# Adaptive-modulation weights laid out by output feature: a VectorE multiply-and-sum per 128 features instead of a VectorE multiply-add per input block with a TensorE column sum

## The chip, the core and the metric

The kernel runs on one core of one Trainium2 chip. The metric is the device time of one execution in microseconds (us). PE is TensorE, DVE is VectorE, ACT is ScalarE, POOL is GpSimd, and SP is the engine whose queue issues nearly all DMAs.

## What is computed

Two layers of a decoder trunk on 256 tokens of width 1024. Each layer takes six vectors of 1024 values from a conditioning vector `c`, and uses them as shift, scale and gate of its two sub-layers:

```
mod = silu(c) @ ada_w[l] + ada_b[l]        # ada_w[l]: 1024 x 6144, float32
h = RMSNorm(x) * (1 + scale_m) + shift_m
... mixer: one projection h @ w_in[l], three branches (RWKV-7, SSD, FoX), merged @ w_out[l]
x = x + gate_m * merged
h = RMSNorm(x) * (1 + scale_f) + shift_f
x = x + gate_f * FFN(h)                    # layer 0 dense SwiGLU, layer 1 top-2-of-8 experts
```

Only the first line is computed in another way after the change. Everything is float32. A product that needs full precision is made of three matmuls on a high and a low part.

## The kernel before

**The big products.** All weights stream from HBM through a ring of three 1 MB tiles `raw` (`raw_piece`, `load_raw`). Each piece of `raw` is split by ACT into `hi` (L156) and by DVE into `lo = raw - hi` (L157, `split_part`), and PE multiplies both with the split activations (`mm3`). So each projection needs DVE before PE, and a ring slot is free for the next DMA once DVE has read it. A mixer layer runs projections, recurrent scan and attention interleaved by the table `ORDER`; then follow `project_out`, and the dense FFN (layer 0) or the experts (layer 1). The scan of `rwkv_half` begins with 32x32 transposes on DVE (L654). What stands before them on DVE is needed first.

**The modulation.** 48 parts of 128 features a layer, 6 vectors of 8. The weights come as the reference has them, input feature by row. The first two vectors of layer 0 (scale and shift of the mixer) are needed before anything else: `first_load` brings them in eight DMAs of 1 MB, and `first_half` multiplies them on PE with `silc` (silu of `c`, one column per 128 inputs) in groups, brings the result to SBUF with ACT, and sums over partitions with four matmuls against `ones` of one column each; `mod_put` adds the bias. The other 20 halves (512 features each) are spread over the program by `mod_next`, which the steps `mo` and `md` of `ORDER` call, and `ffn` after each of its steps: `mod_load` issues the DMAs (tile `araw`, two buffers; for `md` eight tiles of the ring `u` at once), `mod_add`/`mod_sum` makes eight DVE operations of 128x512 on one accumulator, the first a TENSOR_SCALAR (L223), then seven SCALAR_TENSOR_TENSOR (L225), and `mod_finish` sums the accumulator over partitions on PE by four one-column matmuls against `ones` and adds the bias. Six of the halves lie in layer 0's mixer, nine in the FFN, five in layer 1's mixer. The accumulators of the mixer layers are tiles of the ring `u` (15 buffers), which the scan and the attention use too.

**What sets the order.** The code is traced in program order; then a scheduler chooses the order on each engine, within the dependencies and the buffers that are free. Each engine and SP's queue then run strictly in that order.

Of the kernel before, what the change touches and what calls it, by code (L numbers as in the profile page):

```python
# [63 lines left out]
def trunk(  # L64
    ctx: ExitStack, tc: tile.TileContext,
    x, cols, heads, dtw, ada_w, w_in, lora_up, lora_g, rw_v_down, rw_v_up, proj_rw, proj_ssd, proj_fox, w_out,
# [117 lines left out]
    silc = const("silc", [P, KD])  # L184
    cth = const("cth", [P, KD])
    act.activation(cth, pcol[:, 0:KD], AF.Tanh, scale=0.5)
    dve.scalar_tensor_tensor(cth, cth, 1.0, pcol[:, 0:KD], op0=ALU.add, op1=ALU.mult)
    dve.tensor_scalar_mul(silc, cth, 0.5)
# [4 lines left out]
    def mod_put(l, part, half, ps):  # L193
        o = part * 8 + half * 4
        return dve.tensor_tensor(mods[l][part][:, half * 4:half * 4 + 4], ps, adab[l][:, o:o + 4], op=ALU.add)

    mod_raw, mod_late, norm_end = [], [], []

    def mod_load(sc, deep):

        l, part, half = mod_queue.pop(0)
        c0 = part * D + half * 512
        raws = []
        for k0 in range(0, KD, 1 if deep else 2):
            if deep:
                raw = sc("u", [P, 1, 512], bufs=NUNIT)
            else:
                raw = sc("araw", [P, 2, 512], bufs=2)
            with tc.issue_after(loads[2].ins):
                nc.sync.dma_start(raw, rows(ada_w[l], k0 * P, raw.shape[1] * P, c0, 512))  # L210
            raws += [raw[:, i, :] for i in range(raw.shape[1])]
        mod_raw.append((raws, (l, part, half)))

    def mod_add(sc, raws, key):

        with tc.issue_after(norm_end[-1].ins):
            mod_sum(sc, raws, key)

    def mod_sum(sc, raws, key):
        for kt, raw in enumerate(raws):  # L220
            if kt == 0:
                acc = sc("u", [P, 512], bufs=NUNIT) if sc is mx else sc("macc", [P, 512], bufs=3)
                dve.tensor_scalar_mul(acc, raw, silc[:, kt:kt + 1])  # L223
            else:
# [14 lines left out]
    FIRST = [(p, h) for p in (1, 0) for h in range(2)]  # L239
    araws, last_raw = [], []  # L240

    def first_load(n):
        p, h = FIRST[n // 2]
        raw = raw_piece(4, 512) if n < 3 or n == 7 else mx("b8", [P, 4, 512], bufs=NB8)
        last_raw.append(nc.sync.dma_start(raw, rows(ada_w[0], (n % 2) * 512, 512, p * D + h * 512, 512)))
        araws.append(raw)

    def first_half(n):
        ps = sbank()
        for kg in range(2):  # L250
            for q in range(4):
                mm(ps[32 * q:32 * q + 32, :], silc[:, 4 * kg + q:4 * kg + q + 1].broadcast_to([P, 32]), araws[2 * n + kg][:, q, :], kg == 0, kg == 1)
        acc = mx("u", [P, 512], bufs=NUNIT)
        act.activation(acc, ps, AF.Copy, scale=1.0 / 32)
        ps = dbank()
        for j in range(4):
            mm(ps[:, j:j + 1], acc[:, j * P:(j + 1) * P], ones[:, 0:1])
        return mod_put(0, *FIRST[n], ps[:, 0:4])

# [22 lines left out]
    def load_lora(l):  # L282
        up = keep("up", [P, 2, RW])
        nc.sync.dma_start(up, lora_up[l].rearrange("p (a w) -> p a w", a=2))
        gu1 = keep("gu1", [32, RW])
        nc.sync.dma_start(gu1, lora_g[l])
        return up[:, 0, :], up[:, 1, :], gu1

    mod_queue = [(l, p, h) for l, parts in ((0, (2, 4, 3, 5)), (1, (1, 0, 2, 4, 3, 5))) for p in parts for h in range(2)]

    def mod_next(sc, left, deep=False):
        if len(mod_late) > 1:
            mod_finish(mbank if sc is mx else sbank)
        if deep and mod_raw:
            mod_add(sc, *mod_raw.pop(0))
        if len(mod_queue) > left:
            mod_load(sc, deep)
        if not deep and mod_raw:
            mod_add(sc, *mod_raw.pop(0))

    def mod_flush(sc):
        while mod_raw:
            mod_add(sc, *mod_raw.pop(0))
        while mod_late:
            mod_finish(mbank if sc is mx else sbank)
# [153 lines left out]
    def rwkv(mx, l, prm, lora):  # L459
        pp, pph, omu, c2 = prm["pp"], prm["pph"], prm["omu"], prm["c2"]  # L460
        wa = mx("wa", [P, T], bufs=1 + (l > 0))
        gl = mx("gl", [P, 2, T], bufs=1 + (l > 0))
# [548 lines left out]
    def ffn(ff, w_gu, w_down, gf):  # L1011
# [30 lines left out]
        for s in range(steps):  # L1042
# [4 lines left out]
            if s == 8:  # L1047
                mod_flush(ff)
# [449 lines left out]
```

## Time and profile before

| | |
|---|---|
| three runs | 2223.58, 2232.92, 2234.73 us (median 2232.92) |
| profiled execution | 2224.52 us, its span 2222.8 us |
| busy PE / DVE / ACT / POOL | 95% / 81% / 62% / 7% of the span |
| DMA | 546.68 MB, 246 GB/s mean |
| stages in the span | start to 35, layer 0 mixer to 500, FFN to 700, layer 1 mixer to 1175, experts to the end |

A busy share is an average over stages with different limits. What matters for an edit is which engine another waits for in the stage where the edit falls, so the stages are read one by one. An engine works through its queue in order: an instruction that stands in front of another delays it even where nobody needs the first one yet.

### The profile page before, as it was taken

The numbers are of one execution on the slowest core, as the hardware profiler recorded it, in microseconds if no ns is written. First come the engines' busy times: TensorE is split into PE (matmuls) and PEld (weight loads), VectorE is DVE, ScalarE is ACT, GpSimd is POOL, SyncE is SP. The second block draws the span as 40 slices with busy tenths as digits, with TensorE's granted clock in tenths as the row PEclk, the third lists the DMA queues.
The fourth block names the chain that finished last, engine by engine and source line by source line (L and its number), as shares of the span: only waits on it lengthen the run. The fifth ranks groups of instructions, "written<-read, shape, count | busy, mean of one in ns | idle before, by whom it ended". The sixth has DMA issues, their size and how long they took to land.

```text
span 2222.8 us, 35724 instructions
## 1 busy us (share of the span) xinstructions
PE 2115.0 (95%) x13489; PEld 1811.2 (81%) x13489; DVE 1798.8 (81%) x2822; ACT 1386.1 (62%) x2204; POOL 152.1 (7%) x180
## 2 busy tenths in 40 slices
PE   7899899999998889989998999999999999999998
PEld 4777789998997877868998788888888887888776
DVE  4977776777776797756768999999999989999887
ACT  3454455555454545434555877878878777878775
POOL 2211200000000031211002000000000000000000
PEclk9999999999999998988998999999999999999999
DMA  8423254667884533414556999999999999999994
GB/s 304 128 83 95 77 172 156 213 198 259 294 286 137 145 108 93 138 53 130 184 176 251 337 362 359 324 368 367 374 337 352 355 362 336 342 364 368 336 363 151
DMA packets 316101, 546.68 MB, mean 246 GB/s; under 512 B 11952, under 2 KB 143536, under 8 KB 315920
## 3 DMA queue, kind: packets, MB, share of 16 engines
q1 hardware_dynamic: 315920, 544.31, 71.1%
q8 instruction: 108, 1.77, 0.3%
q14 instruction: 73, 0.60, 0.1%
HBM read 543.22 MB, written 1.05 MB: 245 GB/s over the span
## 4 chain that ended last, share of the span: by engine, by line
PE 79%; DVE 13%; issue 3%; ACT 2%; DMA 2%; POOL 0%; SPq 0%; DVEq 0%; ACTq 0%; POOLq 0%
PE pd L122 37%; PE pm L122 33%; PE ps L122 7%; DVE lo L157 5%; PE pm L131 1%; DVE u L654 1%; DMA araw<-in_ada_w_dram 1%; PE ps L131 1%; ACT hi L156 1%; DMA b<-in_ada_w_dram 1%; DVE cu L802 1%; DVE xr L1257 1%; DVE u L225 0%; DMA raw<-in_moe_w_gu_dram 0%; DVE b L612 0%
## 5 line engine op out<-in xcount | busy, mean ns | idle before, releaser
L156 ACT ACTIVATE hi<-raw 128x1024 fp32r<-128x1024 f32 (+2 forms) x1201 | 1027.7, 870 | 522.4 <-PE pd L122 277.0
L157 DVE TENSOR_TENSOR lo<-raw,hi 128x1024 fp32r<-128x1024 f32 (+2 forms) x1197 | 1154.6, 990 | 211.6 <-ACT hi L156 189.8
L122 PE MATMUL pd<-hh,hi 128*128 128x256 f32 (+2 forms) x1208 | 352.7, 293 | 15.3 <-ACT hh L362 3.9
L122 PE MATMUL pd<-hh,lo 128*128 128x256 f32 (+2 forms) x1208 | 346.5, 287 | 0.0
L122 PE MATMUL pd<-hl,hi 128*128 128x256 f32 (+2 forms) x1208 | 345.7, 286 | 0.3
L122 PE MATMUL pm<-lo,hh 128*128 128x512 f32 x672 | 266.7, 397 | 3.0 <-DVE lo L157 2.8
L122 PE MATMUL pm<-hi,hh 128*128 128x512 f32 x672 | 266.9, 397 | 0.1
L122 PE MATMUL pm<-hi,hl 128*128 128x512 f32 x672 | 263.0, 392 | 0.0
L122 PEld LDWEIGHTS pd<-hh,hi 128*128 128x128 f32 (+2 forms) x1208 | 231.9, 192 | 28.3 <-issue 5.6
L122 PEld LDWEIGHTS pd<-hh,lo 128*128 128x128 f32 (+2 forms) x1208 | 231.5, 192 | 6.1 <-issue 3.9
L122 PEld LDWEIGHTS pd<-hl,hi 128*128 128x128 f32 (+2 forms) x1208 | 232.7, 193 | 4.3 <-issue 2.3
L122 PE MATMUL pd<-lo,hi 128*128 128x512 f32 x448 | 174.7, 390 | 0.0
L122 PE MATMUL pd<-hi,hi 128*128 128x512 f32 x448 | 170.9, 391 | 0.1
L122 PE MATMUL pd<-hi,lo 128*128 128x512 f32 x448 | 167.8, 389 | 0.0
L122 PEld LDWEIGHTS pm<-lo,hh 128*128 128x128 f32 x672 | 126.8, 189 | 32.1 <-DVE lo L157 5.5
L122 PEld LDWEIGHTS pm<-hi,hh 128*128 128x128 f32 x672 | 126.5, 188 | 29.3 <-ACT hi L156 1.4
L122 PEld LDWEIGHTS pm<-hi,hl 128*128 128x128 f32 x672 | 126.7, 189 | 26.5
L122 PE MATMUL pm<-hi,more 128*128 128x512 f32 x448 | 142.1, 392 | 0.0
L122 PEld LDWEIGHTS pd<-hi,hi 128*128 128x128 f32 x448 | 84.1, 188 | 18.4 <-ACT hi L405 0.5
L122 PEld LDWEIGHTS pd<-hi,lo 128*128 128x128 f32 x448 | 84.1, 188 | 17.8
L122 PEld LDWEIGHTS pd<-lo,hi 128*128 128x128 f32 x448 | 84.1, 188 | 17.6
L122 PEld LDWEIGHTS pm<-hi,more 128*128 128x128 f32 x448 | 84.1, 188 | 17.5 <-ACT hi L156 0.3
(423 smaller groups left out, 3467.0 us busy)
## 6 DMA issues: line engine op xcount, KB each, us to landing
raw<-in_moe_w_gu_dram SPq DMA_DIRECT2D x224, 1024.0 KB, 7.0
raw<-in_moe_w_down_dram SPq DMA_DIRECT2D x110, 1024.0 KB, 6.8
raw<-in_w_in_dram SPq DMA_DIRECT2D x66, 1024.0 KB, 5.4
araw<-in_ada_w_dram SPq DMA_DIRECT2D x68, 512.0 KB, 4.3
raw<-in_ffn_w_gu_dram SPq DMA_DIRECT2D x22, 1024.0 KB, 6.8
raw<-in_ffn_w_down_dram SPq DMA_DIRECT2D x11, 1024.0 KB, 6.5
raw<-in_w_in_dram SPq DMA_DIRECT2D x16, 512.0 KB, 5.1
raw<-in_proj_ssd_dram SPq DMA_DIRECT2D x8, 1024.0 KB, 5.2
```

The source lines that it names most:

```text
L122: pe.matmul(o, lhsT, rhs, start=start, stop=stop)
L131: pe.transpose(o, i, ident[:n, :n])
L156: act.activation(hi, raw, AF.Copy)
L157: minus.tensor_sub(lo, raw, hi.bitcast(F32))
L654: dve.transpose(blk(bds[ch], q)[:, odd, bcol(q)], by4(blk(pz, q))[:, odd, :])
L802: dve.scalar_tensor_tensor(cu[:, s:T], ps[:, 0:T - s], pph[:, w:w + 1], cu[:, s:T], op0=ALU.mult, op1=ALU.add)
L1257: dve.tensor_add(xr[:, t, hs], xr[:, t, hs], po)
```

## The change

The weights `ada_w` are laid out with the output feature as row, so 128 features are 128 partitions with their 1024 inputs along the free dimension. A new tile `crow` holds `c` as a row on all partitions (one DMA of 512 KB to SBUF, then silu in place by ACT and DVE). One DVE instruction, `tensor_tensor_reduce`, multiplies a 128x1024 tile with `crow`, scales by 0.5 and sums along the row, starting from the bias, into one column of `mods`. The order shows it as ISA of 128x1024 and a second ISA of 128x1 that writes the sum out. There are 96 of them: 16 at the start, 24 in layer 0's mixer, 36 in the FFN, 20 in layer 1's mixer. The matmuls, the ACT copies, the accumulators and the 160 DVE operations of before are gone, `first_half`, `mod_put` and `mod_finish` with them. `mo` and `md` now do the same: up to four loads of 512 KB through the two buffers of `araw`, each followed by the sum of the load before it. `crow` later serves as scratch of the experts (`yw`, `rsb`), `rw_v_up` is loaded with the other small weights, and some small tiles share buffers.

```diff
+    crow = keep("crow", [P, D])
+    nc.sync.dma_start(crow, c_row.partition_broadcast(P))
...
+    def mod_sum(raw, l, part, j):
+
+        dve.tensor_tensor_reduce(raw, raw, crow, 0.5, adab[l][:, part * 8 + j:part * 8 + j + 1], ALU.mult, ALU.add, mods[l][part][:, j:j + 1])
+
+    def mod_load(sc):
+        l, part, j = mod_queue.pop(0)
+        raw = sc("araw", [P, D], bufs=2)
+        with tc.issue_after(loads[2].ins):
+            nc.sync.dma_start(raw, ada_w[l][part * D + j * P:part * D + (j + 1) * P, :])
+        mod_raw.append((raw, l, part, j))
...
-    def mod_sum(sc, raws, key):
-        for kt, raw in enumerate(raws):
-            if kt == 0:
-                acc = sc("u", [P, 512], bufs=NUNIT) if sc is mx else sc("macc", [P, 512], bufs=3)
-                dve.tensor_scalar_mul(acc, raw, silc[:, kt:kt + 1])
-            else:
-                dve.scalar_tensor_tensor(acc, raw, silc[:, kt:kt + 1], acc, op0=ALU.mult, op1=ALU.add)
-        mod_late.append((acc, *key))
-
-    def mod_finish(bank):
-        if mod_late:
-            acc, l, part, half = mod_late.pop(0)
-            ps = bank()
-            for j in range(4):
-                mm(ps[:, j:j + 1], acc[:, j * P:(j + 1) * P], ones[:, 0:1])
-            mod_put(l, part, half, ps[:, 0:4])
...
     def first_load(n):
...
+        p, m = 1 - n % 2, n // 2
+        raw = raw_piece(2, D) if n < 3 or n == 7 else mx("b8", [P, 2, D], bufs=NB8)
+        last_raw.append(nc.sync.dma_start(raw, rows(ada_w[0], p * D + m * 256, 256, 0, D)))
+        for i in range(2):
+            mod_sum(raw[:, i, :], 0, p, 2 * m + i)
...
+    mod_queue = [(l, p, h) for l, parts in ((0, (2, 4, 3, 5)), (1, (1, 0, 2, 4, 3, 5))) for p in parts for h in range(8)]
+
+    def mod_next(sc, left):
+
+        for _ in range(4):
+            if len(mod_queue) > 4 * left:
+                mod_load(sc)
+            if len(mod_raw) > (len(mod_queue) > 4 * left):
+                mod_add()
```

**DVE in the first part of layer 0's mixer.** Before, between the `lo` splits of the second and third projection weight stand the small operations of a softplus (`sm`) and of the masks (`ztm`):

```order
L157 TENSOR_TENSOR lo_641<-raw_603,hi_640 128x512
L426 SCALAR_TENSOR_TENSOR sm_1298<-sm_1298,sm_1296 128x16
L427 SCALAR_TENSOR_TENSOR sm_1328<-sm_1328,sm_1324 128x32
L1370 TENSOR_TENSOR ztm_351<-u_352,ustr 128x128
L427 SCALAR_TENSOR_TENSOR sm_1298<-sm_1298,sm_1294 128x16
L157 TENSOR_TENSOR lo_657<-raw_603,hi_656 128x512
L428 TENSOR_SCALAR sm_1324<-sm_1312 128x32
```

After, the new instructions stand among them, ahead of the first split of the third weight and behind it:

```order
L1326 TENSOR_TENSOR u_314<-u_306,u_295 128x128
L195 ISA araw_2768,mod_8_88<-araw_2768,crow_84,pcol 128x1024
L195 ISA mod_8_88 128x1
L380 RECIPROCAL sm_1236<-sm_1236 128x16
L382 TENSOR_TENSOR sm_1269<-sm_1264,sm_1266 128x32
L1323 COPY u_317<-pm_321 128x128
L157 TENSOR_TENSOR lo_629<-raw_625,hi_628 128x512
L195 ISA araw_2771,mod_8_88<-araw_2771,crow_84,pcol 128x1024
L195 ISA mod_8_88 128x1
L1327 TENSOR_TENSOR ztm_313<-u_314,ustr 128x128
```

All 24 sums of this layer now stand ahead of the scan's first transposes; before, 8 of the layer's 48 operations did, and the other 40 stood further on, among the attention and the merge.

**SP's queue at the same place.** Before, two `araw` loads stand here and then none for seven weights:

```order
L148 DMA raw_532<-in_w_in_dram 128x8x256
L210 DMA araw_874<-in_ada_w_dram 128x2x512
L210 DMA araw_876<-in_ada_w_dram 128x2x512
L148 DMA raw_603<-in_w_in_dram 128x8x256
L148 DMA raw_674<-in_w_in_dram 128x8x256
L809 DMA raw_1357<-in_w_in_dram 128x8x128 x2
L148 DMA raw_1441<-in_w_in_dram 128x8x256
L148 DMA raw_1584<-in_w_in_dram 128x8x256
```

After, they stand among the same weights:

```order
L201 DMA araw_825<-in_ada_w_dram 128x1024
L148 DMA raw_483<-in_w_in_dram 128x8x256
L201 DMA araw_827<-in_ada_w_dram 128x1024
L148 DMA raw_554<-in_w_in_dram 128x8x256
L148 DMA raw_625<-in_w_in_dram 128x8x256
L201 DMA araw_830<-in_ada_w_dram 128x1024
L201 DMA araw_833<-in_ada_w_dram 128x1024
L201 DMA araw_2762<-in_ada_w_dram 128x1024
L201 DMA araw_2765<-in_ada_w_dram 128x1024
L770 DMA raw_1302<-in_w_in_dram 128x8x128 x2
```

From the third on, an `araw` load waits until the sum two before it has read its buffer, and the weights behind it wait with it. In layer 1's mixer it is the same: all 20 sums and loads stand in its first part. PE's order of projections is the same before and after.

**PE in the FFN.** Before, once a step, the four column sums stand between two products:

```order
L122 MATMUL pm_6142<-lo_6858,fah_6621 128x512
L122 MATMUL pm_6142<-hi_6857,fal_6622 128x512
L122 MATMUL ps_6867<-ones,macc_6475 128x1 x4
L122 MATMUL pd_6892<-hh_6041,hi_6893 128x256
L122 MATMUL pd_6892<-hl_6042,hi_6893 128x256
```

After, no row of PE reads a sum; the products follow each other.

## Rows read from the trace of the kernel before

**Rows 1.** The page's busy times and the chain that ended last, by engine.

```profile
PE 2115.0 (95%) x13489; PEld 1811.2 (81%) x13489; DVE 1798.8 (81%) x2822; ACT 1386.1 (62%) x2204; POOL 152.1 (7%) x180
...
PE 79%; DVE 13%; issue 3%; ACT 2%; DMA 2%; POOL 0%; SPq 0%; DVEq 0%; ACTq 0%; POOLq 0%
```

**Rows 2.** Groups of DVE by form: names, shapes, count, busy us, mean ns, idle before.

```profile
L157 DVE TENSOR_TENSOR lo<-raw,hi 128x1024 fp32r<-128x1024 f32 x668 | 788.0, 1220 | 58.1 <-ACT hi L156 43.6
L157 DVE TENSOR_TENSOR lo<-raw,hi 128x512 fp32r<-128x512 f32 x524 | 364.6, 703 | 150.2 <-ACT hi L156 142.8 <-PE pd L122 3.3 <-PE pm L131 0.5
L225 DVE SCALAR_TENSOR_TENSOR macc<-araw,silc,macc 128x512 f32<-128x512 f32 x63 | 47.1, 748 | 16.2 <-DMA araw<-in_ada_w_dram 15.9
```

**Rows 3.** Tiles u: count, duration ns min/median/max, first and last start us.

```profile
L654 DVE STREAM_TRANSPOSE u<-pm x160: 228/309/324, 109.1 to 972.2; 32x128 f32<-32x128 f32 x128, 32x64 f32<-32x64 f32 x32
...
L122 PE MATMUL pm<-ones,u x88: 164/250/352, 296.8 to 1131.6; 128*128 128x1 f32 x88
...
L225 DVE SCALAR_TENSOR_TENSOR u<-araw,silc,u x56: 728/744/1653, 87.6 to 1078.7; 128x512 f32<-128x512 f32 x56
```

**Rows 4.** Timeline of the start: start us, duration us, engine, line, operation.

```profile
6.70 1.94 PE L122 MATMUL ps<-raw,silc 128*32 128x512 f32 x8 [6.70 <-DMA raw<-in_ada_w_dram]
...
26.08 0.16 DVE L336 TENSOR_REDUCE sm<-sm 128x2 f32<-128x8 f32 x1 [5.68 <-ACT ps L335]
26.16 0.15 DVE L195 TENSOR_TENSOR mod<-pd,pcol 128x4 f32<-128x4 f32 x1
...
28.47 0.88 DVE L361 SCALAR_TENSOR_TENSOR h<-pm,ma,u 128x256 f32<-128x256 f32 x2 [2.02 <-ACT u L352]
...
29.93 1.93 PE L122 MATMUL ps<-raw,silc 128*32 128x512 f32 x8 [0.72 <-DMA raw<-in_ada_w_dram]
...
37.63 0.88 DVE L363 SCALAR_TENSOR_TENSOR hl<-h,mod,hh 128x256 fp32r<-128x256 f32 x2
```

**Rows 5.** Busy time by stretch: its length, PE, PEld, DVE, ACT, POOL, PEclk, DMA, GB/s.

```profile
40.00:110.00 70.00, 60.53 (x456) 52.93 (x454) 63.92 (x169) 32.14 (x69) 14.96 (x16) 0.95 0.48 140
...
300.00:500.00 200.00, 198.18 (x1671) 187.40 (x1670) 143.95 (x278) 114.71 (x252) 5.62 (x7) 1.00 0.58 186
550.00:680.00 130.00, 130.00 (x932) 121.75 (x931) 103.57 (x169) 63.37 (x104) 0.00 (x0) 1.00 0.85 283
720.00:770.00 50.00, 46.09 (x376) 42.45 (x374) 37.06 (x109) 31.07 (x65) 2.01 (x1) 1.00 0.53 151
770.00:800.00 30.00, 24.86 (x162) 19.43 (x164) 29.04 (x51) 11.79 (x32) 11.55 (x11) 0.94 0.47 139
```

**Rows 6.** Line L225 alone in stretches: length, DVE busy us (count), PEclk, DMA share, GB/s.

```profile
40.00:110.00 70.00, 6.86 (x7) 0.95 0.48 140
...
550.00:680.00 130.00, 34.04 (x46) 1.00 0.85 283
...
770.00:800.00 30.00, 7.04 (x7) 0.94 0.47 139
```

**Rows 7.** Line L223 alone in two of these stretches.

```profile
40.00:110.00 70.00, 0.48 (x1) 0.95 0.48 140
...
770.00:800.00 30.00, 0.47 (x1) 0.94 0.47 139
```

**Rows 8.** Timeline of PE in an FFN step around the column sums.

```profile
569.53 0.95 PE L122 MATMUL ps<-ones,macc 128*128 128x1 f32 x8
570.34 0.36 PE L122 MATMUL pd<-hh,hi 128*128 128x256 f32 x1
```

**Rows 9.** Tile araw: time from issue to landing of its 68 DMAs.

```profile
DMA to landing us min/median/max: 3.5/4.3/8.6
```

**Rows 10.** The chain of waits in layer 1: start us, us, what.

```profile
873.44 0.43 DVE u L746
873.87 3.33 DVE u L223
877.20 0.03 issue
```

**Rows 11.** Stretch behind the first part of layer 0, columns as in Rows 5.

```profile
110.00:150.00 40.00, 34.35 (x351) 28.10 (x351) 31.34 (x86) 19.29 (x52) 8.19 (x13) 0.91 0.25 76
```

More of the change, by code (lines that the diff above doesn't have):

```diff
@@ L183, in trunk @@
     adab = [pcol[:, KD + 48 * l:KD + 48 * l + 48] for l in range(2)]
[L184 to L188, printed above, removed]
-    mods = [[keep(f"mod{l}{p}", [P, KD]) for p in range(6)] for l in range(2)]
-    def mod_put(l, part, half, ps):
-        o = part * 8 + half * 4
-        return dve.tensor_tensor(mods[l][part][:, half * 4:half * 4 + 4], ps, adab[l][:, o:o + 4], op=ALU.add)
@@ L197, in trunk @@
[L197 to L206, printed above, removed]
-            else:
[L208 to L212, printed above, removed]
@@ L237, in trunk, with mod_add @@
+    def mod_load(sc):
[4 more added lines that the diff above has]
+        mod_raw.append((raw, l, part, j))
+    def mod_add():
+        with tc.issue_after(norm_end[-1].ins):
+            mod_sum(*mod_raw.pop(0))
     stack = ExitStack()
     mx = Scope("mix0", stack)
-    FIRST = [(p, h) for p in (1, 0) for h in range(2)]
-    araws, last_raw = [], []
@@ L242, in first_load @@
-    def first_load(n):
[L243 to L258, printed above, removed]
+    for half in range(2):
+        hs = slice(half * 512, half * 512 + 512)
+        cth = mx("u", [P, 512], bufs=NUNIT)
+        act.activation(cth, crow[:, hs], AF.Tanh, scale=0.5)
+        dve.scalar_tensor_tensor(crow[:, hs], cth, 1.0, crow[:, hs], op0=ALU.add, op1=ALU.mult)
@@ L260, in make_params @@
+    last_raw = []
+    def first_load(n):
+        p, m = 1 - n % 2, n // 2
[3 more added lines that the diff above has]
+            mod_sum(raw[:, i, :], 0, p, 2 * m + i)
     def make_params(l):
@@ L284, in load_lora, with mod_flush @@
         nc.sync.dma_start(up, lora_up[l].rearrange("p (a w) -> p a w", a=2))
-        gu1 = keep("gu1", [32, RW])
-        nc.sync.dma_start(gu1, lora_g[l])
+        gu1 = keep("gu1", [64, RW])
+        nc.sync.dma_start(gu1[0:32], lora_g[l])
+        if l > 0:
+            nc.sync.dma_start(gu1[32:64], rw_v_up)
         return up[:, 0, :], up[:, 1, :], gu1
[L289 to L301, printed above, removed]
+    mod_queue = [(l, p, h) for l, parts in ((0, (2, 4, 3, 5)), (1, (1, 0, 2, 4, 3, 5))) for p in parts for h in range(8)]
[5 more added lines that the diff above has]
+                mod_add()
+    def mod_flush():
         while mod_raw:
-            mod_add(sc, *mod_raw.pop(0))
-        while mod_late:
-            mod_finish(mbank if sc is mx else sbank)
+            mod_add()
     def mod_row(dgs, l, part, scale, row, bank=dbank):
@@ L460, in rwkv @@
         pp, pph, omu, c2 = prm["pp"], prm["pph"], prm["omu"], prm["c2"]
-        wa = mx("wa", [P, T], bufs=1 + (l > 0))
-        gl = mx("gl", [P, 2, T], bufs=1 + (l > 0))
+        wa = mx("wa", [P, T])
+        gl = mx("gl", [P, 2, T])
         def shift(dst, ps, i):
@@ L1047, in ffn @@
             if s == 8:
-                mod_flush(ff)
+                mod_flush()
             if s == 5:
@@ L1092, in moe @@
         iota = ff("iota", [P, P])
-        iotai = ff("iotai", [P, P], I32)
+        iotai = keep("h32", [P, P], I32, bufs=2)
         pool.iota(iotai, pattern=[[1, P]], base=0, channel_multiplier=0)
@@ L1383, in trunk @@
                     y_fox, fx = fox(mx, l, prm, dtr)
-                elif step == "mo":
-                    mod_next(mx, 0)
-                elif step == "md":
-                    mod_next(mx, MOD_LEFT[l], True)
+                elif step in ("mo", "md"):
+                    mod_next(mx, MOD_LEFT[l])
                 elif step == "gm":
-                    while mod_late and mod_late[0][2] == 2:
-                        mod_finish(mbank)
-                    gm = keep("vfirst", [P, 2, 512]) if l == 1 else mx("u2", [P, 2, 512])
-                    gm = [gm[:, 0], gm[:, 1]]
+                    if l == 0:
+                        gm = [unit(mx, 1, 512)[:, 0, :] for _ in range(2)]
+                    else:
+                        gm = keep("vfirst", [P, 2, 512])
+                        gm = [gm[:, 0], gm[:, 1]]
                     mod_row(lambda: unit(mx, 4, P), l, 2, 0.5, gm)
@@ L1407, in trunk @@
             hh, hl = pair("hh", "hl")
-            mod_flush(mx)
+            mod_flush()
             for j in range(0, KD, 2):
@@ L1472, in lay_out @@
     put["rw_v_down"] = by_partition(inputs["rw_v_down"][0])
+    put["c_row"] = _np.reshape(inputs["c"], -1)
+    put["ada_w"] = inputs["ada_w"].transpose(0, 2, 1)
     put["moe_router"] = by_partition(inputs["moe_router"][0])
```

24 lines of the change are left out of this document (8 added, 16 removed).

## The prediction

> **What bounds the kernel now.** I read the page's busy times and the chain that ended last first: PE is busy 95% of the span and carries 79% of the chain, DVE 13% [rows 1]. So an edit is worth what it takes from PE where PE never waits, and costs what it adds to DVE where PE waits for DVE. Then I read the stretches. From 300 to 500 and from 550 to 680 us PE has 198.18 of 200 and 130 of 130 us: DVE time saved there buys nothing, PE time saved there buys all of itself. In the first part of layer 0's mixer, 40 to 110 us, it is the other way round: DVE is busy 63.92 of 70 us, PE 60.53 [rows 5]. The scan's transposes begin at 109.1 us [rows 3], at the end of that stretch, so what DVE does before them comes straight ahead of the scan. In layer 1 the same part is 720 to 800 us, DVE 37.06 of 50 and 29.04 of 30 [rows 5].
>
> **One new instruction.** No tensor_tensor_reduce is in this trace. Its nearest row is the subtraction of two 128x1024 float32 tiles, 1.22 us [rows 2]. The written sum is a second small instruction; two small ones that do not wait start 0.08 us apart, 26.08 and 26.16 us [rows 4]. I take 1.22 + 0.08 = 1.30 us, with 1.4 us as the upper end (0.16 us for the small one). The pair of an old half, one 0.48 us operation [rows 7] and seven of 0.748 us [rows 2], is 5.7 us; four new ones are 5.2 us. So on DVE as a whole almost nothing changes after the start: 20 x 5.7 = 114 us become 80 x 1.30 = 104 us. What changes is where they stand.
>
> A row and a rule disagree on the price. An operation with two float32 sources in SBUF and a pointer scalar took 748 ns for 512 elements, the plain subtraction 703 ns [rows 2]: 45 ns more, not twice. The Trainium skill, "Vector Engine (DVE) Microarchitecture Reference", section "Points that are easy to get wrong", says that such an operation whose two SBUF sources are not bf16 runs at half throughput. By it the new instruction would take about twice the subtraction; what that would do is the third rival below.
>
> **The start: +6 us.** The eight 1 MB pieces arrive from 6.70 to 29.93 us [rows 4], with 1 MB of x and 0.5 MB of small weights between them: 8.5 MB in 23.2 us, 2.7 us a MB. The row of `c` on 128 partitions is 0.5 MB more ahead of them: the last lands 1.4 us later, at 31.3 us. Two sums a piece take 2.6 us, less than a piece takes to land, so DVE keeps up, and only the last two lie behind the last landing: 33.9 us. Then it costs more: before, the scale was complete early, and the eight operations `h` of the norm began at 28.47 us and the last `hl` ended at 38.5 us [rows 4]. Now the order has all of them behind the last sum. About 1 us of small ones, eight `h` and eight `hl` at 0.44 us [rows 4] and five splits of at most 0.7 us [rows 2] make 11 us, so they end at about 45 us. That is 6.5 us later; the projections that begin in this time run on with what is there, so I take 6, bounds 3 and 8.
>
> **Layer 0's mixer: +18 us.** All 24 sums stand ahead of the scan. DVE's other work in 40 to 110 us is 63.92 - 6.86 - 0.48 = 56.6 us [rows 5 to 7]; with 24 x 1.30 = 31.2 it is 87.8 us in a stretch of 70. If every idle microsecond is filled, DVE reaches the scan 17.8 us later; if the 6.1 us of idle time stay, 23.9. Some of these run while POOL is busy too, where the old ones took up to 1653 ns instead of 744 [rows 3], +3 us at most. What can give some back is the next stretch, 110 to 150 us, with 8.7 us of DVE idle [rows 11], but these are waits inside the scan, PE to DVE and back, that move along. I take 18, bounds 17.8 - 8.7 = 9 and 23.9 + 3 = 27. DVE's saving later in the layer, 40 operations, falls where PE is at 99% [rows 5]: nothing.
>
> **Layer 1's mixer: +10 us.** The 20 sums (26 us) now stand in 720 to 770 us. DVE's work in 720 to 800 is 66.1 us, less 7.04 + 0.47 us of old ones [rows 5 to 7]: 58.6 + 26 = 84.6 us in 80. With all idle time filled that is 4.6 us late, with all 13.9 us of it kept 18.5. The buffers agree with the middle: a buffer of `araw` turns round in 1.3 us of sum, 4.3 us of DMA [rows 9] and some 0.2, so two buffers give a sum each 2.9 us: 20 need 58 us, 8 to 10 more than the stretch of 720 to 770. I take 10.
>
> **FFN and the finish: -19 us.** PE's column sums start at 569.53 and the next product at 570.34: 0.81 us a half [rows 8]. Nine lie in the FFN where PE is never idle: -7.3 us. Eleven lie in the mixers, 88 matmuls [rows 3], where PE is at 99%: -8.9 us. And in layer 1 the chain has a first multiply of 3.33 us instead of 0.48, with PE waiting behind it [rows 10]: -2.9 us. Together -19, bounds -12 (some of the mixer's stand in waits, and the long multiply hides another wait) and -22. DVE's own FFN share is 36 x 1.30 = 47 for nine halves of 5.7 = 51 us, hidden under PE as before. The four PE sums and ACT copies of the start lie under the landing of the weights: nothing.
>
> **Sum:** 6 + 18 + 10 - 19 = +15 us; bounds 3 + 9 + 4.6 - 22 = -5 and 8 + 27 + 18.5 - 12 = +41. On the profiled execution's 2224.52 us that is 2240. Its time is at the lower end of the runs shown (2223.58, 2232.92, 2234.73), so I add to the mean of the four, 2228.9: **2244 us**, 2224 to 2270 by its own bounds.
>
> **Rivals.**
> 1. *DVE's queue absorbs it (no change).* The stretch 40 to 110 us is full of small operations on masks and softplus, and the order moved some of them behind the splits. If PE's backlog of projections covers half of the delay in layer 0 (9) and layer 1's is the least (4.6), then 4 + 9 + 5 - 19 = -1: 2228 us. For it speaks PE's 86% in that stretch, against it DVE's 91% and that all of it precedes the scan.
> 2. *Faster: only PE's column sums count.* If PE has enough ready work in both mixers that no delay of DVE reaches the scan, and only the later landing at the start remains: 3 - 19 = -16, 2213 us. It decides at a delay under about 8 us over start and mixers together; above that the gain is not more than 0.5%. Against it: it needs DVE to do 31 us more in a place where it has 6 us.
> 3. *The new instruction is half as fast,* 2 x 1.22 + 0.08 = 2.5 us. Then a piece at the start takes 5.0 us of DVE and not 2.7 us of landing, and the eight end at 6.7 + 8 x 5.0 = 47 us instead of 34 (+13); the mixers pay 24 x 1.2 = 29 and 20 x 1.2 = 24 more; in 550 to 680 us DVE would have 103.57 - 34 - 3 + 26 x 2.5 = 131.6 us for 130 (+2). With the +15: 83 us, 2312 us. The 748 ns row speaks against it [rows 2]. The Trainium skill's sentence named above is what speaks for it.
>
> **How the numbers follow.** A measurement of this kernel can tell about 0.5%, 11 us. The forecast has 0.57, of which 0.15 falls within 0.5% (its sum under +11). The first rival has 0.17, all within. The second has 0.17, of which 0.15 faster and 0.02 within. The third has 0.09. So faster 0.15, same 0.34, slower 0.51. The range reaches from the middle of the second rival, 2213, to just above the forecast's upper end, 2274; it leaves out the third rival and half of the second, and holds 0.8.
>
> **What would show it.** In the profile after, one 128x1024 sum of 1.2 to 1.4 us (the third rival: 2.4) 96 times; DVE at 95% or more between 45 and about 130 us with PE idle 25 us or more there; the first transposes at about 133 us instead of 109.1; the same in layer 1, with its scan about 10 us later against the end of the FFN; and an FFN about 7 us shorter with PE at 100%. I would be wrong if the first transposes stand under 120 us, since then the delay was absorbed, or if the new sums wait for their DMAs by several microseconds each, since then it is more than the sum says.

## The result: 1.2% slower, and the profile after

The changed kernel took 2258.8 us (median of five runs, 2249.88 to 2260.8) against 2230.11 us (five runs of the kernel before, 2223.58 to 2234.73). The ratio estimated from these runs is 1.0122, 95% interval 1.0093 to 1.0150. The profiled execution is 2249.88 us with a span of 2248.2 us, 25.4 us more than the span before. By the medians the difference is 28.7 us; the two profiled executions lie 8.9 and 5.6 us under their medians. The forecast was slower by 15 us, 2244 us.

The page's busy times and its chain, as in [rows 1]:

```profile
PE 2096.9 (93%) x13233; PEld 1801.5 (80%) x13233; DVE 1809.9 (81%) x2830; ACT 1379.4 (61%) x2201; POOL 156.7 (7%) x180
...
PE 76%; DVE 14%; DMA 4%; issue 3%; ACT 2%; SPq 0%; POOL 0%; DVEq 0%; ACTq 0%; POOLq 0%
```

PE is busy 18 us less than in [rows 1], and the kernel is 25 us longer: PE waits 43 us more. DVE's total grew by 11 us only, its share of the chain by a point, and DMA's from 2% to 4%.

DVE's groups by form, the new sum beside the subtraction that priced it in [rows 2]:

```profile
L157 DVE TENSOR_TENSOR lo<-raw,hi 128x1024 fp32r<-128x1024 f32 x668 | 786.4, 1220 | 55.8 <-ACT hi L156 43.3
...
L195 DVE CUSTOM_DVE_ANT_0 araw<-araw,crow,pcol 128x1024 f32<-128x1024 f32 x80 | 103.6, 1299 | 30.5 <-DMA araw<-in_ada_w_dram 30.4
```

Tile `u` (count, duration ns min/median/max, first and last start), the row that answers [rows 3]:

```profile
L615 DVE STREAM_TRANSPOSE u<-pm x160: 227/309/324, 133.9 to 1007.7; 32x128 f32<-32x128 f32 x128, 32x64 f32<-32x64 f32 x32
```

The scan's first transposes come at 133.9 instead of 109.1 us. Line L195 (the sums) alone, by stretch: length, DVE busy with its instruction count (two per sum), granted clock, DMA share, GB/s. The answer to [rows 6]:

```profile
40.00:135.00 95.00, 32.20 (x48) 0.86 0.68 219
135.00:523.00 388.00, 0.00 (x0) 0.96 0.38 117
543.00:706.00 163.00, 42.60 (x66) 1.00 0.85 290
726.30:832.20 105.90, 25.62 (x40) 0.85 0.62 199
```

All 24 sums of layer 0 lie ahead of the scan and none in the 388 us behind it; all 20 of layer 1 lie between the FFN and its scan.

To see where the time went I cut both traces at the same events, and give each stretch from start to end: to the scan's first transposes; to those of its second half; to the first addition of the output projection; (the projection itself is 14.1 us in both); from the projection's last addition to the FFN's last; then for layer 1 the first three again. Columns as in [rows 5]. The kernel before:

```profile
0.00:109.10 109.10, 87.67 (x601) 67.44 (x601) 73.31 (x201) 45.72 (x106) 27.59 (x49) 0.92 0.66 213
109.10:225.30 116.20, 104.40 (x916) 89.55 (x917) 87.10 (x205) 57.94 (x141) 22.10 (x28) 0.94 0.31 92
225.30:484.80 259.50, 252.09 (x2163) 228.98 (x2162) 183.64 (x380) 139.03 (x309) 22.40 (x26) 0.98 0.52 164
498.90:705.10 206.20, 198.94 (x1411) 185.55 (x1411) 158.68 (x265) 101.98 (x176) 0.70 (x1) 0.99 0.76 252
705.10:800.60 95.50, 81.06 (x598) 70.13 (x598) 74.69 (x181) 49.35 (x114) 17.80 (x16) 0.93 0.49 145
800.60:944.70 144.10, 134.73 (x1134) 115.71 (x1130) 112.75 (x243) 72.52 (x167) 27.99 (x31) 0.93 0.37 109
944.70:1177.50 232.80, 220.57 (x1859) 198.35 (x1860) 152.93 (x315) 117.99 (x261) 22.02 (x27) 0.94 0.45 141
```

The changed kernel:

```profile
0.00:133.90 133.90, 81.66 (x505) 70.62 (x505) 117.92 (x269) 44.40 (x103) 34.10 (x50) 0.90 0.75 253
133.90:250.50 116.60, 103.90 (x918) 89.26 (x918) 86.14 (x204) 57.37 (x139) 22.24 (x28) 0.96 0.29 86
250.50:510.80 260.30, 250.04 (x2110) 227.44 (x2111) 160.99 (x335) 139.48 (x311) 20.32 (x25) 0.95 0.42 128
524.90:726.30 201.40, 192.36 (x1339) 176.44 (x1339) 154.00 (x256) 100.25 (x176) 0.70 (x1) 0.99 0.76 258
726.30:832.20 105.90, 83.92 (x584) 74.50 (x585) 89.69 (x209) 47.75 (x111) 19.09 (x16) 0.85 0.62 199
832.20:978.80 146.60, 134.91 (x1152) 116.08 (x1151) 110.81 (x241) 75.01 (x174) 31.26 (x34) 0.93 0.32 94
978.80:1206.40 227.60, 216.89 (x1812) 193.47 (x1813) 136.85 (x284) 116.49 (x258) 17.29 (x23) 0.93 0.39 121
```

Read the first numbers down the two fences: +24.8, +0.4, +0.8, -4.8, +10.4, +2.5, -5.2 us. Everything behind them (projection, experts, end) is 3.5 us shorter. The two stretches ahead of a scan carry +35 us. Three stretches hold the old column sums (layer 0's third, the FFN and layer 1's last), and layer 1's second holds the long first multiply of [rows 10]. Together these four should have paid back 19 us, and they pay back 6.7 (0.8 - 4.8 + 2.5 - 5.2).

### The profile page after: what moved, and what is told of

It is laid out like the page before. It is cut to its first block, busy times and chain, and to the rows that moved or that the text cites. A ratio compares the mean times of both kernels' runs of the same rounds, so it can differ in the third digit from the quotient of the medians.

```text
span 2248.2 us, 35159 instructions
## 1 busy us (share of the span) xinstructions
PE 2096.9 (93%) x13233; PEld 1801.5 (80%) x13233; DVE 1809.9 (81%) x2830; ACT 1379.4 (61%) x2201; POOL 156.7 (7%) x180
## 4 chain that ended last, share of the span: by engine, by line
PE 76%; DVE 14%; DMA 4%; issue 3%; ACT 2%; SPq 0%; POOL 0%; DVEq 0%; ACTq 0%; POOLq 0%
PE pd L122 35%; PE pm L122 32%; PE ps L122 6%; DVE lo L157 5%; DMA araw<-in_ada_w_dram 3%; DVE araw L195 2%; PE pm L131 2%; DVE u L615 1%; PE ps L131 1%; DMA b<-in_ada_w_dram 1%; ACT hi L156 1%; DVE cu L763 1%; DVE xr L1218 0%; DMA raw<-in_moe_w_gu_dram 0%; DVE h L1127 0%
## 5 line engine op out<-in xcount | busy, mean ns | idle before, releaser
L195 DVE CUSTOM_DVE_ANT_0 araw<-araw,crow,pcol 128x1024 f32<-128x1024 f32 x80 | 103.6, 1299 | 30.5 <-DMA araw<-in_ada_w_dram 30.4
```

The lines of the kernel that those rows point to most:

```text
L195: dve.tensor_tensor_reduce(raw, raw, crow, 0.5, adab[l][:, part * 8 + j:part * 8 + j + 1], ALU.mult, ALU.add, mods[l][part][:, j:j + 1])
```

## Experiments

Two questions stood after the result. Is it the place of the sums in DVE's queue that costs 35 us? And where did two thirds of the expected saving go? The table gives all twelve kernels, cut as above. "s1" is the scan's first half, "rest" from its second half to the projection. Ratios are to the kernel before on the same chip (medians 2229.79, 2229.35 and 2228.05 us in the three groups of later runs). The ratios are of all runs, but the stretches of a row are of the one execution that was profiled, and no two groups were on the same chip. It lies within 1.2 us of its kernel's median for spread, oldspread, bufs, oldlate and late4; under it by 3.1 us for late2, 4.4 for late, 5.6 for before, 5.9 for nocol, 8.9 for changed and 9.1 for late3; and above it by 8.8 us for short.

| kernel | ratio (95%) | start to scan | s1 | rest | FFN | layer 1: to scan | s1 | rest |
|---|---|---|---|---|---|---|---|---|
| before | 1 | 109.1 | 116.2 | 259.5 | 206.2 | 95.5 | 144.1 | 232.8 |
| before2 (again) | one profile | 108.6 | 116.2 | 259.4 | 206.4 | 95.4 | 147.2 | 233.2 |
| changed | 1.0122 (1.0093-1.0150) | 133.9 | 116.6 | 260.3 | 201.4 | 105.9 | 146.6 | 227.6 |
| short | 0.9930 (0.9914-0.9946) | 109.6 | 128.1 | 254.2 | 197.1 | 94.6 | 154.0 | 225.5 |
| spread | 1.0010 (0.9997-1.0024) | 114.0 | 124.9 | 257.1 | 196.2 | 94.3 | 155.0 | 230.6 |
| nocol (old layout) | 1.0010 (0.9996-1.0024) | 109.6 | 115.4 | 253.3 | 209.0 | 105.9 | 142.3 | 230.2 |
| late | 1.0007 (0.9993-1.0020) | 103.3 | 121.6 | 264.5 | 195.9 | 96.3 | 147.5 | 239.9 |
| oldspread (old layout) | 1.0023 (1.0010-1.0035) | 108.9 | 116.1 | 260.0 | 208.3 | 96.7 | 147.2 | 234.1 |
| bufs | 1.0123 (1.0108-1.0139) | 132.0 | 119.3 | 261.2 | 197.8 | 107.7 | 150.6 | 228.9 |
| late2 | 0.9956 (0.9940-0.9973) | 104.1 | 114.4 | 270.4 | 195.1 | 90.6 | 150.2 | 230.7 |
| oldlate (old layout) | 1.0091 (1.0076-1.0107) | 108.0 | 118.3 | 271.4 | 213.0 | 87.4 | 150.0 | 244.2 |
| late3 | 0.9929 (0.9915-0.9942) | 103.8 | 114.3 | 257.2 | 196.0 | 87.4 | 150.0 | 232.6 |
| late4 | 0.9942 (0.9928-0.9955) | 103.2 | 118.1 | 264.4 | 195.5 | 87.3 | 152.5 | 233.4 |

### Is it DVE's time, and its place?

**short**: the later sums become a read of one column.

```diff
-        dve.tensor_tensor_reduce(raw, raw, crow, 0.5, adab..., ALU.mult, ALU.add, mods[l][part][:, j:j + 1])
+        if first:
+            dve.tensor_tensor_reduce(raw, raw, crow, 0.5, adab..., ALU.mult, ALU.add, mods[l][part][:, j:j + 1])
+        else:
+            dve.tensor_scalar(mods[l][part][:, j:j + 1], raw[:, 0:1], 0.5, None, op0=ALU.mult)
```

> The changed kernel, in which the 80 sums after the first 16 only read one column of their tile (128x1, the multiply-and-sum over 1024 elements is left out); the loads, the buffers and the order rules stay. Theory (DVE's time ahead of the scan): 24 x 1.25 = 30 us go from DVE's queue in layer 0 and 25 us in layer 1. The first transposes come at 105 to 113 us instead of 133.9 (the start's 3.6 us stay), layer 1's come 93 to 97 us after the end of the FFN instead of 105.9, and the whole is 30 to 40 us under the changed kernel: 2210 to 2220, a ratio to the kernel before of 0.990 to 0.997. Rival (the transfers and SP's queue delay the projections, DVE only shows it): the loads are all still there, so the first transposes stay at 128 us or later and the ratio at 1.008 to 1.013.

Measured: 2213.7 us, 0.993. The first transposes are back at 109.6 us, layer 1's at 94.6 us behind the FFN, both inside the theory's ranges. By the medians the whole is 45 us under the changed kernel, more than the 30 to 40 expected. The loads are all still there, nearly in the same places of SP's queue, so the rival falls. Short also frees the loads' buffers sooner, but that could win back no more than the time in which DVE stood idle: in the changed kernel 4.8 of the 95 us from 40 to 135, 2.4 of them before sums that waited for their loads. It is DVE's own time ahead of the scan.

But in this execution not all that came back stayed. The scan's first half took 128.1 us instead of 116.6. Three rows of this run, the stretch as a whole and two pieces of it:

```profile
109.60:237.70 128.10, 118.39 (x918) 98.82 (x918) 88.11 (x207) 57.00 (x139) 22.73 (x29) 0.84 0.26 79
...
184.00:206.00 22.00, 19.72 (x167) 19.34 (x166) 20.46 (x47) 14.62 (x29) 3.21 (x5) 1.00 0.47 144
206.00:234.00 28.00, 27.65 (x94) 19.84 (x93) 12.42 (x23) 4.06 (x8) 6.06 (x6) 0.51 0.13 38
```

The same 918 matmuls, in another order, kept PE busy for 118.39 us here and for 103.90 us in the changed kernel. The granted clock was 0.84 against 0.96. In the last piece it is 0.51, so PE was at the lower of its two levels, 1.2 GHz, almost throughout; in the piece before, it was at 2.4 GHz. The same kind of product (`pd`, 128x256) starts every 0.12 us at 202 us and every 0.21 us at 212 us. So 11.5 of the 24.3 us won ahead of the scan were given back inside it. How much of that the other executions pay is not shown: the profiled one, at a mean clock of 0.961, took the longest of six, and the other five had 0.963 to 0.970.

**spread**: one rule altered. A sum may be queued only behind the latest weight split written before it.

```diff
-        minus.tensor_sub(lo, raw, hi.bitcast(F32))
+        last = minus.tensor_sub(lo, raw, hi.bitcast(F32))
+        if minus is dve:
+            lows.append(last)
...
-        with tc.issue_after(norm_end[-1].ins):
+        with tc.issue_after(lows[-1].ins):
             mod_sum(*mod_raw.pop(0))
```

> The changed kernel with one rule altered: a later sum may enter DVE's queue only behind the latest weight split written before it, not behind the first norm. Same sums, loads and buffers; 3 instead of 24 sums then stand ahead of layer 0's first transposes. Theory (place, not price): the first transposes come at 104 to 112 us instead of 133.9 and layer 1's 93 to 98 us after the FFN instead of 105.9; the rest keeps the after's savings, so 28 to 38 us under the changed kernel, 2212 to 2222, ratio to the kernel before 0.991 to 0.998. Rival 1 (the sums cost what they cost, wherever they stand): the delay moves to the second half of the scan or to the gates, ratio 1.008 to 1.013. Rival 2 (the new layout saves nothing that PE feels): the delay goes, and the start's 4 us stay, ratio 1.000 to 1.003.

Measured: 2231.15 us, 1.001. The place theory holds where it speaks: 114.0 us (2 over its range) and 94.3 us behind the FFN, with every sum still computed and at the same price. Its total fails. The number is rival 2's, but not for rival 2's reason: the FFN is 10 us shorter than before. What was lost instead is in the scans' first halves, +8.7 and +10.9 us. Part of this is work that moved there from ahead of the scan: 958 and 1175 matmul records against 916 and 1134 before. So a part of the earlier first transposes is only moved as well. The rest goes with the clock, 0.90 and 0.91 where the kernel before had 0.94 and 0.93. Length times clock, a rough measure of the work, grew by 3 and 7 us only. Over all runs spread's mean clock is 0.962 (12 runs) and that of the kernel before 0.966 (29 runs).

**before2**: is that clock chance?

> The kernel before once more, for a second profile: how far do the lengths of its stretches differ between two executions of one program? If the program's order sets the granted clock of a stretch, the stretches (109.1, 116.2, 259.5 us in layer 0, 206.2 us in the FFN, 95.5, 144.1, 232.8 us in layer 1) come again within 3 us each and their clocks within 0.03. If it is chance, some differ by 8 us or more, as between nocol and the first profile (95.5 against 105.9 us).

Measured: six of the seven stretches came again within 0.6 us, the seventh (s1 of layer 1) within 3.1 us, and their clocks within 0.02. These two profiles hardly differ, but both lie at the lower end of the kernel's times (2224.52 and 2227.06 us, of 2222.89 to 2239.16), so they do not settle the question. The kernels late, late2, late3 and late4 (below) say more: up to the scan's second half the traces show the same order of instructions in all four, on every engine and in SP's queue. Their s1 of layer 0, 926 matmul records, took 121.6, 114.4, 114.3 and 118.1 us, at clocks of 0.92, 0.97, 0.97 and 0.94. The rows of late and late3:

```profile
103.30:224.90 121.60, 107.49 (x926) 92.55 (x926) 89.79 (x202) 57.76 (x140) 27.89 (x31) 0.92 0.26 79
...
103.80:218.10 114.30, 102.35 (x926) 88.09 (x926) 88.26 (x202) 57.55 (x139) 26.29 (x30) 0.97 0.28 84
```

The groups of runs were on different chips, late in one, late2 in the next, late3 and late4 (3.8 us apart) together in the last. So with one and the same order this stretch can differ by 7 us between two profiles, and a difference of 8 to 12 us in one profile of each kernel is not shown to come from the order. For layer 0's rest the order does show: 0.98, 0.98 and 0.97 in before, before2 and oldspread, which share one order there, and 0.95 twice in changed and bufs, which share another.

### What are the column sums worth?

**nocol**: the kernel before without its column sums.

```diff
-            ps = bank()
-            for j in range(4):
-                mm(ps[:, j:j + 1], acc[:, j * P:(j + 1) * P], ones[:, 0:1])
-            mod_put(l, part, half, ps[:, 0:4])
+            mod_put(l, part, half, acc[:, 0:4])
```

> The kernel before without its four column-sum matmuls per half: the 20 later halves take the first four columns of the accumulator in place of the sums over partitions (the sum over partitions is left out); loads, DVE products and their places stay. It prices the saving by itself. The prediction's sum: 20 x 0.81 = 16 us less, 7.3 of it in the FFN (from the last addition of layer 0's projection to the FFN's end 206.2 us before), ratio 0.991 to 0.994. Rival (the gap read from two starts is partly time in which PE would have waited for something else, as the changed kernel's stages say): 5 to 9 us less, 4 to 5 of it in the FFN, ratio 0.996 to 0.998.

Measured: 2231.77 us, 1.001. Neither expectation: nothing is gained at all. The pieces say more than the sum, though the order of the other instructions moved too when the column sums went. Layer 0's rest, at the same clock of 0.98, is 6.2 us shorter, more than its six halves at 0.81 us. The FFN is 2.8 us longer although 72 matmul records are gone from it. Its waits (us in total, times, longest):

```profile
DVE macc L225 <- DMA araw<-in_ada_w_dram: 23.5, 16, 3.9
...
PEld pm L122 <- DVE lo L157: 9.3, 7, 3.1
...
PE pm L122 <- DVE lo L157: 6.6, 5, 2.8
```

The same waits in the kernel before (517 to 690 us; nocol's are from 510 to 690):

```profile
DVE macc L225 <- DMA araw<-in_ada_w_dram: 14.6, 15, 4.1
...
PEld pm L122 <- DVE lo L157: 1.8, 1, 1.8
...
PE pm L122 <- DVE lo L157: 1.3, 1, 1.3
```

A product waits at the head of DVE's queue for its transfer; the weight splits `lo` stand behind it, and PE waits for them. And the front of layer 1 is 10.4 us longer with nearly the same work in it, at a clock of 0.84 against 0.93:

```profile
701.30:807.20 105.90, 89.36 (x606) 77.86 (x606) 79.68 (x185) 49.00 (x114) 18.18 (x16) 0.84 0.45 135
```

PE is busy 8.3 us longer there than before and idle 2.1 us longer, so this is mostly the clock. Whether the order or this one execution lowered it is not shown.

**bufs**: does the changed kernel's FFN lose its saving in that way?

```diff
-        raw = sc("araw", [P, D], bufs=2)
+        raw = sc("araw", [P, D], bufs=2 if sc is mx else 4)
```

> The changed kernel with four buffers instead of two for the weight tiles of the FFN's sums, nothing else. Theory (in the changed kernel the FFN's sums wait in DVE's queue for tiles whose buffer came free too late, 22.3 us over 18 waits, and weight splits stand behind them): the waits fall under 8 us, the FFN from 201.4 to 196 to 198 us, ratio to the kernel before 1.008 to 1.011. Rival (the transfers themselves are the limit, DMA share 0.92 to 0.97): the waits move to the weights' own tiles, the FFN stays at 200 us or more, ratio 1.011 to 1.014.

Measured: 2256.41 us, 1.0123; FFN 197.8 us. The FFN's waits in the changed kernel:

```profile
DVE araw L195 <- DMA araw<-in_ada_w_dram: 21.1, 17, 2.5
...
PEld ps L122 <- DVE lo L157: 3.2, 5, 1.3
PEld pd L122 <- DVE lo L157: 2.1, 5, 0.8
PE ps L122 <- DVE lo L157: 2.1, 4, 1.1
```

With four buffers the first of these rows is not among its waits any more, and the FFN saves 8.4 us against the kernel before instead of 4.8. So the local theory holds and its rival (the transfers are the limit) falls. The whole did not get faster, and its ratio is the rival's: layer 1's front and the first half of its scan together took 5.8 us more than in the changed kernel's profile, with an order of their own.

**oldspread**: the rule of spread in the old layout (the same diff around the old `mod_sum`).

> The kernel before with the rule of the run spread: a product of a half may enter DVE's queue only behind the latest weight split written before it. Layout, products, column sums and loads as before. Theory (the column sums cost PE what their gap says, and the run nocol lost its gain in the FFN to weight splits queued behind products that wait for their loads): no such waits, so each FFN step with a half takes 16.75 + 0.81 to 0.91 us, the FFN 202 to 205 us (206.2 before, 196.2 in spread), the whole 0.996 to 1.000 of the kernel before. Rival (spread's FFN of 196.2 us comes from the rule, not from the new layout): the FFN takes 199 us or less here too.

Measured: 2234.92 us, 1.0023; FFN 208.3 us. Neither expectation: the theory's FFN was 202 to 205 us, the rival's 199 or less. The rule gives the old layout nothing, so spread's 196.2 needs the new layout; under the same rule the two are 12 us apart in the FFN. An FFN step without column sums takes 16.75 us from one activation (tile `fa` on ACT) to the next in spread; those with column sums in oldspread take 17.64 to 17.66. That is 0.9 us a half, or 8 us for nine; most of the rest lies in one step of 23.67 us.

### Where the sums fit

**late** and **late2** use spread's rule and write the mixers' sums behind the scans. In late, layer 0's second part holds 36, the FFN 12 and layer 1's second part 32; in late2 it is 24, 36 and 20. Late2's order is:

```diff
-        "rw r0 r0 mo r0 r0 fx sd s0 s0 s0 s1 s1 s1 r1 r1 r1 r0 s2 mo s2 s2 f0 r1 r1 s3 mo G f0 mo G s3 s3 G "
-        "f0 G m0 f1 m0 f1 m0 md md m1 md m0 m1 m1 md f1 md md md m1 m2 gm m2 md m2 m2"
+        "rw r0 r0 r0 r0 fx sd s0 s0 s0 s1 s1 s1 r1 r1 r1 r0 s2 s2 s2 f0 r1 r1 s3 G f0 G s3 s3 G "
+        "f0 G m0 md f1 m0 f1 md m0 md m1 m0 m1 md m1 f1 md m1 m2 md gm m2 m2 m2"
...
-        "rw r0 r0 mo r0 sd s0 s0 r0 r0 s0 s1 mo s1 s1 s2 r1 r1 G r1 s2 fx r1 G s2 r1 G s3 s3 mo f0 f0 s3 G m0 "
-        "f0 m0 mo m0 m0 f1 md f1 m1 m1 md md md gm m1 md m1 f1 m2 m2 m2 md md md m2"
+        "rw r0 r0 r0 sd s0 s0 r0 r0 s0 s1 s1 s1 s2 r1 r1 G r1 s2 fx r1 G s2 r1 G s3 s3 f0 f0 s3 G m0 "
+        "f0 m0 m0 md m0 f1 md f1 m1 md m1 md gm m1 md m1 f1 m2 m2 m2 m2"
```

> The changed kernel with the sums spread as in the run spread, and the written order moved: no sum before the end of either scan, 36 sums in layer 0's second part (300 to 500 us), 12 instead of 36 in the FFN, 32 in layer 1's second part. Theory: DVE is busy 14 to 18 of 25 us there and the DMA share is 0.4 to 0.5, so 36 x 1.25 = 45 us fit; the scans start at 104 to 112 us, and an FFN with 12 instead of 18.9 MB... 6.3 instead of 18.9 MB of these loads loses the waits for the tile (22 us over 18 waits on DVE, 4.8 us less PE idle): 0 to 6 us under the run spread, ratio to the kernel before 0.988 to 0.996. Rival (PE waits for DVE in the second part once the sums are there): that part grows by 5 us or more, ratio 0.998 to 1.005.

> The changed kernel with the rule of spread and all of the mixers' sums written behind the scans: 24 in layer 0's second part, 36 in the FFN, 20 in layer 1's second part. Theory (place decides, and 24 and 20 sums fit where 36 and 32 in the run late added 5 and 7 us): first transposes at 103 to 106 us, from the second transposes to layer 0's projection 254 to 259 us (264.5 in late), the FFN 196 us, layer 1's second part 225 to 231 us (239.9 in late); ratio to the kernel before 0.987 to 0.996. Rival (what the delays give back, TensorE's lower clock in the scans takes): the mean granted clock stays at 0.964 or less against 0.966 of the kernel before, and the ratio is 0.998 to 1.002.

Measured: late 2231.59 us, 1.0007; late2 2220.2 us, 0.9956. Late went as its rival said: the second parts grew by 5.0 and 7.1 us. With the scans' first halves (+5.4 and +3.4) they ate what the first front (-5.8) and the FFN (-10.3) gave. Two thirds of the FFN's loads less gained it only 0.3 us over spread, so their amount was not its limit. Late2 beats both kernels, but its rest of layer 0, forecast at 254 to 259, is 270.4 us.

**late3** and **late4** differ from late2 in layer 0's line alone. Of its second part, late3:

```diff
-        ... s3 s3 G f0 G m0 md f1 m0 f1 md m0 md m1 m0 m1 md m1 f1 md m1 m2 md gm m2 m2 m2
+        ... s3 s3 md G f0 md G m0 md f1 m0 md f1 m0 md md m1 m0 m1 m1 f1 m1 m2 gm m2 m2 m2
```

late4 spreads its groups one to every three or four steps (`md G f0 G m0 md f1 m0 f1 md m0 md m1 m0 md m1 m1 md f1 ...`).

> As the run late2, but layer 0's 24 sums stand in the first half of its second part, as in the run late, and not among its last steps. Theory (late2 lost 11 us from the second transposes to the projection, 270.4 against 259.5 us, by sums among the last steps, where PE waits for the splits behind them): this stretch takes 257 to 264 us, the whole 0.990 to 0.995 of the kernel before. Rival (any 24 sums there cost it by the granted clock, 0.95 against 0.98): 267 us or more, ratio 0.995 to 0.998.

> As the run late3, but its six groups of four sums stand one to every three or four steps of layer 0's second part. Theory (it is the crowding that costs: four groups in a row put 8 sums ahead of a split): from the second transposes to the projection 255 to 262 us, ratio 0.989 to 0.995. Rival (crowding is no cost, only the last steps are): the same as late3 within 2 us.

Measured: late3 2212.15 us, 0.9929; late4 2215.21 us, 0.9942. Late3's whole is inside its theory's range and, with its interval, under the rival's. Its 257.2 us fits the theory too, but in an execution 9.1 us under the median of five that reach from 2203.03 to 2216.51. Late4's rest of 264.4 us fits neither of its expectations. The rows of that stretch in late3 and late4:

```profile
218.10:475.30 257.20, 246.63 (x2110) 223.92 (x2111) 186.80 (x384) 138.74 (x311) 22.61 (x25) 0.98 0.55 174
...
221.30:485.70 264.40, 252.64 (x2110) 228.66 (x2111) 185.84 (x384) 139.01 (x311) 21.06 (x25) 0.95 0.53 169
```

Both have 2110 matmul records, and length times clock is 252 us for late3 and 251 us for late4. What separates these two executions is the clock, not a wait. The medians are only 3.1 us apart and the intervals overlap, so it is not shown that the two orders differ, and why the clock fell in one of the executions stays open.

**oldlate**: late2's order and rule in the old layout.

> The kernel before with the written order of the run late2 and its rule: the old layout, with all products and column sums of the mixers behind the scans. It asks whose gain late2's 0.9956 is. Theory (the layout's: no column sums, and an FFN of 195 instead of 206 us): here the FFN stays at 205 to 209 us, the first transposes come at 100 to 106 us, the second parts grow by more than that gains; ratio to the kernel before 0.998 to 1.006. Rival (the order's: the same sums behind the scans are better in either layout): 0.997 or less.

Measured: 2249.58 us, 1.0091. The rival falls: this order is bad for the old layout and good for the new one. It is worse than the theory expected too: the ratio, the FFN (213.0 us) and the first transposes (108.0 us) lie above its ranges. The rows of its rest of layer 0, its FFN and its rest of layer 1, each longer than late2's in the table (by 1.0, 17.9 and 13.5 us):

```profile
226.30:497.70 271.40, 257.17 (x2176) 233.21 (x2177) 190.03 (x389) 139.54 (x312) 20.90 (x25) 0.96 0.53 170
511.10:724.10 213.00, 203.25 (x1411) 189.91 (x1411) 155.99 (x266) 102.89 (x176) 0.70 (x1) 0.96 0.74 244
...
961.50:1205.70 244.20, 227.41 (x1864) 203.20 (x1865) 162.68 (x328) 117.33 (x259) 20.28 (x27) 0.92 0.48 156
```

In one written order, the layouts differ by 1.4% (late2 against oldlate, 0.9956 against 1.0091) in favour of the new one. In the order they were given, by 1.2% against it.

## Why the prediction was right, step by step

The direction was right, and so were the two delays that decide it. The size was not: 15 us slower were forecast, and it is 28.7 by the medians and 25.4 by the profiles. Most of the difference is one term, the saving of 19 us.

**The new instruction, 1.30 us.** Right. The sums of tile `araw` took 1258/1282/2181 ns (min/median/max), and with their reads 32.20 us for 24, 1.34 each; forecast 31.2. On DVE's timeline of the start, the first sums, the end of the last one, and the last `hl`:

```profile
9.37 1.29 DVE L195 CUSTOM_DVE_ANT_0 raw<-raw,crow,pcol 128x1024 f32<-128x1024 f32 x1 [1.26 <-DMA raw<-in_ada_w_dram]
10.58 0.08 DVE L195 DVE_READ_ACCUMULATOR2_ANT mod<- 128x1 f32 x1
10.58 1.28 DVE L195 CUSTOM_DVE_ANT_0 raw<-raw,crow,pcol 128x1024 f32<-128x1024 f32 x1
...
34.19 0.08 DVE L195 DVE_READ_ACCUMULATOR2_ANT mod<- 128x1 f32 x1
...
45.36 0.54 DVE L326 SCALAR_TENSOR_TENSOR hl<-h,mod,hh 128x256 fp32r<-128x256 f32 x1 [0.24 <-ACT hh L325]
```

The third rival (2.4 us a sum) falls with the first and third rows: 1.21 us from start to start. The half rate that the Trainium skill states for `S2S2D2_STT` in "Vector Engine (DVE) Microarchitecture Reference", "Points that are easy to get wrong", does not appear for this instruction; the measurement decides.

**The start, +6: mis-sized, +3.6.** The last sum ended at 34.27 us (forecast 33.9) and the last `hl` at 45.90 (forecast 45). The error was in the base. The prediction ended the norm of before at 38.5 us, by the row of [rows 4] that starts at 37.63. That is not the last pair. In the trace of before another ends at 42.27 us:

```profile
41.33 0.94 DVE L363 SCALAR_TENSOR_TENSOR hl<-h,mod,hh 128x256 fp32r<-128x256 f32 x2 [0.18 <-ACT hh L362]
```

Against that the slip is 3.6 us, still inside the bounds of 3 to 8.

**Layer 0, +18.** Start and mixer together were to be +24, and the first transposes are +24.8 us late; without the start's 3.6 the mixer's part is 21, inside 9 to 27. That the two together came out at the forecast 24 is luck: the start was 2.4 us too high and the mixer 3 too low. The stretch it was said to show in:

```profile
40.00:135.00 95.00, 74.00 (x475) 64.53 (x475) 90.24 (x219) 34.09 (x73) 19.48 (x17) 0.86 0.68 219
```

DVE is at 95% and PE idle for 21 us (forecast 25 or more). Nothing was absorbed in the two stretches behind (+0.4 and +0.8), so the first rival falls, and the second with it. Two of the sums took 1.80 and 2.18 us, both while POOL was busy; that is 1.4 of the 3 us allowed for it. That the delay is DVE's time was shown by short, with the same 505 matmul records ahead of the scan, and that it is the place by spread, which also moved 38 of these records behind its first transposes.

**Layer 1, +10.** +10.4 us from the FFN's end to the scan. Short and spread take it back (94.6, 94.3). Nocol has the same 105.9 us without any new sum, but in another way: PE is idle for 16.5 us there, and for 22.0 in the changed kernel against 14.4 before. So 7.6 of the 10.4 us are waits.

**FFN and the rest, -19: the term that failed.** Its parts were -7.3 in the FFN, -8.9 in the mixers and -2.9 for the long first multiply. The changed kernel shows -4.8 in the FFN, and in the mixers behind the first transposes +1.2 (layer 0) and -2.7 (layer 1): -6.3, outside the bounds of -12 to -22. (Against the second profile of before, whose s1 of layer 1 is 147.2 us, it would be about -10, outside too.) The price per half was right: 0.81 forecast, 0.9 where nothing else waits (spread against oldspread). Two things took most of the rest. In the FFN the sums wait for loads with only two buffers, and weight splits stand behind them; with four buffers -8.4. So PE was busy for 192.36 of the FFN's 201.40 us, and not throughout, as forecast. In layer 0's rest the clock was 0.95 instead of 0.98, and 0.95 again in bufs. Length times clock is 247 us against 254, so by this rough measure the work did shrink by 7 us, and the clock took it. That the saving would be had in full wherever PE is at 99% was the wrong step, and nocol, where nothing of it arrives in the total, says so most plainly. What the long multiply alone was worth was not measured.

With the measured terms the sum is 3.6 + 21.2 + 10.4 - 6.3 = +29 instead of +15; the 3.5 us behind layer 1, which no step foresaw and no run looked into, make the 25.4 of the profiles.

## What to carry to other kernels

In an engine's in-order queue, ask where a piece of work will stand before asking what it costs: work that is ready early is put early, and the same sums, which made the stretches ahead of two scans 35 us longer, left the kernel 0.7% faster than before when they stood behind the scans (late3). A saving on the busiest engine is worth its size only if no other queue is waiting at that place too, so look at the waits next in line. And compare two layouts each in an order that suits it: here one order put the new layout 1.2% behind, another 1.4% ahead. And where the clock moves by itself, one profile of each kernel is too little to say which of two orders made a stretch of 110 us 7 us longer.

## What the runs showed of the hardware

TensorE's granted clock is a term as large as many edits here. Over 29 runs of the kernel before, time and mean clock go together (correlation -0.84): 2222.89 us at 0.969 and 2239.16 us at 0.960, 1.3 us for each 0.001 by a fitted line. It goes in part with the order of the instructions: in layer 0's rest 0.98, 0.98 and 0.97 in three profiles of one order, 0.95 in both of another. In part it goes with the execution, or the chip: in the scan's first half 0.92, 0.94, 0.97 and 0.97 for one order, with 121.6, 118.1, 114.4 and 114.3 us. That a gain of DVE ahead of the scan could be half undone by it, as in the profile of short (0.84 against 0.96), was not expected.

Of two DVE multiply-and-sums of 1024 columns in a row, the second starts 1.21 us after the first, though the first lasts 1.29. The read of the first one's sum, 0.08 us, starts together with the second, so it adds no time of its own between them.
